# The up projection of a feed-forward part by Strassen's scheme, in quarters with the down projection

## The chip, the cores and the metric

The kernel runs on one core of a Trainium2 chip. The metric is the device time of one execution in microseconds. Engines are called TensorE (PE in the rows, PEld for its weight loads), VectorE (DVE), ScalarE (ACT), GpSimd (POOL) and SyncE (SP, which issues the loads and stores).

## What is computed

Two layers of an encoder trunk work on 512 tokens of 1024 features, all in float32. The change concerns the feed-forward part that ends each layer:

```python
D_MODEL, SEQ, DEPTH, D_FF = 1024, 512, 2, 4096
...
    for l in range(DEPTH):
        ...
        x = x + merged @ w_out[l]

        h = rms_norm(x, norm_ffn[l])
        x = x + jnp.square(jax.nn.relu(h @ w_ff1[l])) @ w_ff2[l]
```

`merged` is what three attention branches give, gated and summed; its product with `w_out` is the output projection that stands right before the feed-forward part.

## The kernel before

Activations lie feature-major: a tile has 128 features on the partitions and all 512 tokens in its columns, so x is 8 tiles. Every float32 product is made of three matmuls in the float32r type. Each operand is split into a rounded part `hi` and a remainder `lo`, and the three products hi·hi, hi·lo and lo·hi are added up in PSUM. `feature_tile` (line 324) issues these three matmuls for each of the k-tiles of one output tile; each matmul loads a 128x128 block of weights and moves 512 columns. The third of the three is the one that reads the weights' `lo`.

Weights come from one packed array through `Stream.take` (line 127). It loads 128x1024 numbers (eight 128x128 blocks) into a `raw` tile, makes `hi` by a ScalarE copy (line 140) and `lo` by a VectorE subtract (line 142). The tags `raw`, `whi` and `wlo` have three buffers each (pool `w`, line 185). The order of instructions on TensorE is that of the program; on the other engines a scheduler orders them by priority, and the instructions of `take` are moved ahead by 30 places (`high_priority`).

In `merge` (line 880) eight output tiles `ps_o` are computed, each is added to its tile of x, and `norm_part` (line 262) multiplies x by the gain, splits it into `xgh` and `xgl` and adds its square to `acc` on GpSimd. The factor of the norm depends on the token alone; it is worked out later (`norm_sums`, `norm_rows`) and lies in `rb`.

In `ffn` (line 919) two halves follow one another. In each, 16 up tiles are computed (8 k-tiles x 3 = 24 matmuls each). Each goes through relu, the factor `rb` and the square, and is split into `ah` and `al`. Then 8 down tiles take the 16 as their k-tiles (48 matmuls each) and are added to x. The first ups run interleaved, seven of eight steps each, while the last x tile is still being normalized. PSUM has 8 banks: 3 `mm`, 2 `s`, 2 `pt`, 1 `y`.

## Time and profile before

| | |
|---|---|
| median of 3 runs | 1858.28 us (1857.52 to 1861.04) |
| profiled execution, its own time | 1858.96 us |
| its span, first to last instruction | 1856.9 us |
| mean granted TensorE clock | 0.993 |
| TensorE busy | 1801.5 us in 8496 matmuls |
| VectorE, ScalarE, GpSimd busy | 1088.9, 784.5, 311.4 us |

The span is what the rows of the trace cover; the time of the execution is 2.1 us longer. A busy engine is one that has an instruction in it; on TensorE successive matmuls overlap, so that the distance between their starts, not their listed length, is what each adds.

### The profile page before, as it was taken

How to read it: one execution, taken by the hardware profiler on the slowest of the kernel's cores; microseconds unless marked ns; L12 is line 12 of the kernel's file. 1: busy time of each engine (PE TensorE's matmuls, PEld its weight loads, DVE VectorE, ACT ScalarE, POOL GpSimd, SP SyncE). 2: the span in 40 equal slices, each digit the busy share in tenths (PEclk: the TensorE clock that was granted, in tenths of full speed). 3: DMA queues.
4: the chain of work that ended last, by engine and by line, in shares of the span. 5: the costliest groups of instructions: out<-in, count | busy, mean ns of one | idle time of the engine just before them, and what ended most of it. 6: DMA issues, size and time to landing. Idle time of an engine off the chain costs nothing.

```text
span 1856.9 us, 23295 instructions
## 1 busy us (share of the span) xinstructions
PE 1801.5 (97%) x8496; PEld 1495.0 (81%) x8496; DVE 1088.9 (59%) x2223; ACT 784.5 (42%) x1369; POOL 311.4 (17%) x289
## 2 busy tenths in 40 slices
PE   8989989989999999999999899899899999999999
PEld 6778878877888888888887788788778888888887
DVE  7566468488865642454355654684888756334632
ACT  6565456446643221223245644564466433222221
POOL 1442222043101000000124312220431110000000
PEclk9999999999999999999999999999899999999999
DMA  5653365332252333333336533643322533333341
GB/s 180 154 147 105 101 163 138 100 113 69 80 193 80 106 99 98 96 100 110 119 113 158 132 96 109 169 116 110 103 84 80 178 95 97 102 91 102 92 119 62
DMA packets 78850, 211.46 MB, mean 114 GB/s; under 512 B 11392, under 2 KB 14464, under 8 KB 78736
## 3 DMA queue, kind: packets, MB, share of 16 engines
q1 hardware_dynamic: 78736, 209.97, 39.3%
q8 instruction: 67, 1.10, 0.2%
q14 instruction: 47, 0.39, 0.1%
HBM read 172.15 MB, written 12.62 MB: 100 GB/s over the span
## 4 chain that ended last, share of the span: by engine, by line
PE 79%; DVE 8%; ACT 4%; DMA 4%; issue 3%; POOL 2%; SPq 1%; DVEq 0%; ACTq 0%; POOLq 0%
PE ps L331 38%; PE ps_t L366 15%; PE ps_f L331 10%; PE ps_o L331 5%; PE ps_b L776 5%; PE ps_s L662 2%; PE ps_p L689 2%; PE ps_y L700 2%; DMA qq<-nat 2%; DVE pr L677 1%; POOL wlo L142 1%; DVE pr L670 1%; ACT whi L140 1%; DMA cb<-cum 1%; ACT pr L675 1%
## 5 line engine op out<-in xcount | busy, mean ns | idle before, releaser
L140 ACT ACTIVATE whi<-raw 128x1024 fp32r<-128x1024 f32 (+1 forms) x337 | 307.1, 919 | 764.8 <-issue 320.6
L142 DVE TENSOR_TENSOR wlo<-raw,whi 128x1024 fp32r<-128x1024 f32 (+2 forms) x237 | 287.6, 1213 | 232.2 <-ACT whi L140 227.8
L331 PE MATMUL ps<-xgh,whi 128*128 128x512 f32 x512 | 199.4, 389 | 0.0
L331 PE MATMUL ps<-xgh,wlo 128*128 128x512 f32 x512 | 199.2, 389 | 0.0
L331 PE MATMUL ps<-xgl,whi 128*128 128x512 f32 x512 | 199.2, 389 | 0.0
L331 PE MATMUL ps<-ah,whi 128*128 128x512 f32 x512 | 199.2, 389 | 0.0
L331 PE MATMUL ps<-al,whi 128*128 128x512 f32 x512 | 199.2, 389 | 0.0
L331 PE MATMUL ps<-ah,wlo 128*128 128x512 f32 x512 | 199.2, 389 | 0.0
L331 PE MATMUL ps_f<-xgh,whi 128*128 128x512 f32 x464 | 196.2, 423 | 0.0
L331 PE MATMUL ps_f<-xgh,wlo 128*128 128x512 f32 x464 | 182.5, 393 | 0.0
L331 PE MATMUL ps_f<-xgl,whi 128*128 128x512 f32 x464 | 182.5, 393 | 0.0
L142 POOL TENSOR_TENSOR wlo<-raw,whi 128x1024 fp32r<-128x1024 f32 x50 | 121.1, 2422 | 257.0 <-ACT whi L140 234.3
L366 PE MATMUL ps_t<-whi,xgh 128*128 128x512 f32 x384 | 151.2, 394 | 7.0 <-ACT whi L140 7.0
L366 PE MATMUL ps_t<-wlo,xgh 128*128 128x512 f32 x384 | 150.1, 391 | 0.0
L366 PE MATMUL ps_t<-whi,xgl 128*128 128x512 f32 x384 | 149.9, 390 | 0.0
L283 POOL TENSOR_TENSOR acc<-acc,t 128x512 f32<-128x512 f32 x24 | 41.6, 1732 | 518.9 <-ACT t L282 518.9
L331 PEld LDWEIGHTS ps<-ah,whi 128*128 128x128 f32 x512 | 96.1, 188 | 20.1
L331 PEld LDWEIGHTS ps<-xgl,whi 128*128 128x128 f32 x512 | 96.1, 188 | 19.9
L331 PEld LDWEIGHTS ps<-xgh,wlo 128*128 128x128 f32 x512 | 96.1, 188 | 19.9
L331 PEld LDWEIGHTS ps<-al,whi 128*128 128x128 f32 x512 | 96.1, 188 | 19.9
L331 PEld LDWEIGHTS ps<-xgh,whi 128*128 128x128 f32 x512 | 96.1, 188 | 19.9
L331 PEld LDWEIGHTS ps<-ah,wlo 128*128 128x128 f32 x512 | 96.1, 188 | 19.8
(194 smaller groups left out, 3387.0 us busy)
## 6 DMA issues: line engine op xcount, KB each, us to landing
raw<-w SPq DMA_DIRECT2D x277, 512.0 KB, 3.6
qq<-nat SPq DMA_DIRECT2D x64, 128.0 KB, 2.9
kk<-nat SPq DMA_DIRECT2D x64, 128.0 KB, 2.4
kl<-nat SPq DMA_DIRECT2D x64, 128.0 KB, 2.4
gd<-t SPq DMA_DIRECT2D x32, 256.0 KB, 2.2
cb<-cum SPq DMA_DIRECT2D x16, 256.0 KB, 4.0
cb<-gd SPq DMA_DIRECT2D x16, 256.0 KB, 2.7
g<-gd SPq DMA_DIRECT2D x16, 256.0 KB, 4.3
```

Of the source, the lines that this page charges most:

```text
L140: nc.scalar.activation(out=hi[:, c : c + v], in_=raw[:, c : c + v], func=AF.Copy)
L142: k.lo_engine.tensor_tensor(out=lo[:, c : c + w], in0=raw[:, c : c + w], in1=hi[:, c : c + w].bitcast(F32), op=ALU.subtract)
L283: (engine or nc.gpsimd).tensor_tensor(out=self.acc, in0=self.acc, in1=sq, op=ALU.add)
L331: nc.tensor.matmul(out=ps, lhsT=a[:, k], rhs=b[k], start=first and k == 0 and j == 0, stop=last and k == n - 1 and j == 2)
L366: nc.tensor.matmul(out=pss[t][:, 0:width], lhsT=a[k][:, t * P : t * P + P], rhs=b[:, i], start=c == 0 and i == 0 and j == 0, stop=last and ...
L662: nc.tensor.matmul(out=ps[:, 0:n], lhsT=a[:, i * P : (i + 1) * P], rhs=b[:, 0:n], start=j == 0, stop=j == len(terms) - 1)
L670: nc.vector.tensor_tensor_reduce(out=p, in0=ps[:, 0:n], in1=b, scale=1.0, scalar=-3e38 * sign, op0=ALU.add, op1=ALU.max if branch == 2 els ...
L675: nc.scalar.activation(out=p, in_=p, func=AF.Exp, bias=mn, scale=sign, accum_out=ls)
L677: nc.vector.tensor_scalar(out=p, in0=p, scalar1=li, scalar2=None, op0=ALU.mult)
L689: nc.tensor.transpose(ps[:, o + (i - kb) * P : o + (i - kb + 1) * P], pr[:, offs[i] + kb * P : offs[i] + (kb + 1) * P], self.ident)
L700: nc.tensor.matmul(out=yps[:, kb * P : T], lhsT=qkv[2][kb // 2][:, kb % 2, h, :], rhs=head[h][gi][x][:, o : o + T - kb * P], start=gi == 0 ...
L776: nc.tensor.matmul(out=pss[u], lhsT=chunk[a][:, u, k], rhs=y[b][k], start=k == 0 and j == 0, stop=k == 3 and j == 2)
```

## The change

The up projection is computed by Strassen's scheme in Winograd's form. The 1024 features are cut into two halves of 512, the 512 tokens into two halves of 256, and two up tiles (256 columns of `w_ff1`) form a pair, whose two column blocks are 128 wide. Each block product of 512 features x 128 columns x 256 tokens is 4 k-tiles x 3 = 12 matmuls of 256 columns. Seven such products replace the eight of a pair. Before them come sums of weight blocks (`take_pair`: four GpSimd subtracts and four splits, two of which go to tags `twh` and `twl` with two buffers) and sums of activation blocks (`norm_pair`, in place of `norm_part`; the output tiles are computed in the order 0, 4, 1, 5, ...). After them come the sums of products in `pair_sum`.

`ffn` runs in four quarters: four pairs (8 up tiles), then 8 downs over 8 k-tiles (24 matmuls each), each added to x. The factor of the norm is squared (`rb2`) and multiplied in after the downs. The weights of a pair are taken one pair ahead; those of the first pair of a later quarter are taken before the fifth down of the quarter ahead of it. The packing of `w_ff1` follows (`chunk_of`). Lines that are only "..." stand for parts left out.

```diff
+    def take_pair(self, pool, *key):
+        k, nc = self.k, self.k.nc
+        raw = [k.pw.tile([P, 1024], F32, tag="raw", name="raw") for _ in range(2)]
+        sums = [pool.tile([P, 1024], F32, tag="tw", name="tw", bufs=3) for _ in range(2)]
+        w = {}
+        def split(names, src, n, tags):
+            hi, lo = (p.tile([P, 1024], F32R, tag=t, name=t, **b) for p, t, b in tags)
+            nc.scalar.activation(out=hi[:, 0:n], in_=src[:, 0:n], func=AF.Copy)
+            nc.vector.tensor_tensor(out=lo[:, 0:n], in0=src[:, 0:n], in1=hi[:, 0:n].bitcast(F32), op=ALU.subtract)
+            for i, name in enumerate(names):
+                w[name] = tuple(x[:, 512 * i : 512 * i + 512].rearrange("p (k m) -> p k m", m=P) for x in (hi, lo))
+        with k.tc.high_priority(k.ahead):
+            for i in range(2):
+                nc.sync.dma_start(out=raw[i], in_=self.ap[self.layer, :, self.at + 1024 * i : self.at + 1024 * i + 1024])
+            b = [raw[i][:, 512 * j : 512 * j + 512] for i in range(2) for j in range(2)]
+            t = [sums[i][:, 512 * j : 512 * j + 512] for i in range(2) for j in range(2)]
+            sub = lambda out, x, y: nc.gpsimd.tensor_tensor(out=out, in0=x, in1=y, op=ALU.subtract)
+            plain = ((k.pw, "whi", {}), (k.pw, "wlo", {}))
+            summed = ((pool, "twh", dict(bufs=2)), (pool, "twl", dict(bufs=2)))
+            split(["b11"], raw[0], 512, plain)
+            split(["b21", "b22"], raw[1], 1024, plain)
+            sub(t[0], b[1], b[0])
+            sub(t[1], b[3], t[0])
+            split(["t1", "t2"], sums[0], 1024, summed)
+            sub(t[2], b[3], b[1])
+            sub(t[3], b[2], t[1])
+            split(["t3", "t4"], sums[1], 1024, summed)
+        self.at += 2048
+        self.keys.append((2048, key))
         return w
...
-        return dict(s=self.pS, y=self.py, mm=self.mm)[tag].tile([P, T], F32, tag=tag, name=name)
+        return dict(s=self.pS, y=self.py, mm=self.mm, pt=self.pt)[tag].tile([P, T], F32, tag=tag, name=name)
...
+    def norm_pair(self, l, vcol, pool, kt, x):
+        nc = self.nc
+        h2 = T // 2
+        a, b = slice(0, h2), slice(h2, T)
+        g = self.gain(l, vcol + kt)
+        if kt < 4:
+            self.half = self.half if kt else {}
+            t = self.half[kt] = self.tmp()
+            nc.scalar.activation(out=t, in_=x, func=AF.Copy, scale=g)
+            return
+        t = self.half.pop(kt - 4)
+        q = pool.tile([P, 3, h2], F32, tag="sq", name="sq", bufs=1)
+        sub = lambda out, u, v: nc.vector.tensor_tensor(out=out, in0=u, in1=v, op=ALU.subtract)
+        h = self.px.tile([P, T], F32R, tag="xgh", name="xgh")
+        lo = self.px.tile([P, T], F32R, tag="xgl", name="xgl")
+        nc.scalar.activation(out=h, in_=x, func=AF.Copy, scale=g)
+        sub(q[:, 1], t[:, a], t[:, b])
+        nc.vector.scalar_tensor_tensor(out=t[:, b], in0=x[:, b], scalar=g, in1=t[:, b], op0=ALU.mult, op1=ALU.add)
+        sub(q[:, 0], t[:, b], t[:, a])
+        nc.vector.scalar_tensor_tensor(out=q[:, 2], in0=x[:, a], scalar=g, in1=q[:, 0], op0=ALU.mult, op1=ALU.subtract)
+        nc.vector.scalar_tensor_tensor(out=lo, in0=x, scalar=g, in1=h.bitcast(F32), op0=ALU.mult, op1=ALU.subtract)
+        f = {"a12": [y[:, a] for y in (h, lo)], "a22": [y[:, b] for y in (h, lo)]}
+        h = self.px.tile([P, T], F32R, tag="xgh", name="xgh")
+        lo = self.px.tile([P, T], F32R, tag="xgl", name="xgl")
+        nc.scalar.activation(out=h, in_=t, func=AF.Copy)
+        sub(lo, t, h.bitcast(F32))
+        f |= {"a11": [y[:, a] for y in (h, lo)], "s1": [y[:, b] for y in (h, lo)]}
+        h = pool.tile([P, 3, h2], F32R, tag="sh", name="sh", bufs=4)
+        lo = pool.tile([P, 3, h2], F32R, tag="sl", name="sl", bufs=4)
+        nc.scalar.activation(out=h, in_=q, func=AF.Copy)
+        sub(lo, q, h.bitcast(F32))
+        for i in range(3):
+            f[f"s{2 + i}"] = [y[:, i] for y in (h, lo)]
+        self.xf.append(f)
...
-    def norm_rows(self):
-        nc = self.nc
-        ps = self.pt.tile([P, T], F32, tag="pt", name="ps_r")
+    def norm_rows(self, tag=None):
+        nc = self.nc
+        ps = self.bank(tag, "ps_r") if tag else self.pt.tile([P, T], F32, tag="pt", name="ps_r")
...
-    def merge(self, l, y, x):
+    def merge(self, l, y, x, pool):
...
-                self.norm_part(l, V_FFN, m, x[m])
-
-            outs = [out(m) for m in range(KT)]
+                self.norm_pair(l, V_FFN, pool, m, x[m])
+                self.norm_square(m, x[m])
+            self.xf = []
+            outs = [out(m) for m in (0, 4, 1, 5, 2, 6, 3, 7)]
...
+    PRODUCTS = (
+        ("b11", "a11", 0, 0),
+        ("b21", "a12", 1, 0),
+        ("t2", "s2", 1, 1),
+        ("t3", "s3", 2, 0),
+        ("t1", "s1", 2, 1),
+        ("t4", "a22", 3, 0),
+        ("b22", "s4", 3, 1),
+    )
+    def pair_products(self, w, tags, order):
+        nc = self.nc
+        h2 = T // 2
+        ps = [None] * 4
+        for i in order:
+            stationary, moving, bank, half = self.PRODUCTS[i]
+            if ps[bank] is None:
+                ps[bank] = self.bank(tags[bank], f"ps_w{bank}")
+            out = ps[bank][:, half * h2 : half * h2 + h2]
+            hi, lo = w[stationary]
+            n = len(self.xf)
+            for k, f in enumerate(self.xf):
+                xh, xl = f[moving]
+                for j, (a, b) in enumerate(((hi, xh), (hi, xl), (lo, xh))):
+                    nc.tensor.matmul(out=out, lhsT=a[:, k], rhs=b, start=k == 0 and j == 0, stop=k == n - 1 and j == 2)
+            yield
+        self.ps = ps
+    def pair_sum(self, ps, z):
+        nc = self.nc
+        h2 = T // 2
+        add = lambda out, x, y: nc.vector.tensor_tensor(out=out, in0=x, in1=y, op=ALU.add)
+        two = lambda x: x.rearrange("p (u t) -> p u t", u=2)
+        p1 = self.tmp()[:, 0:h2]
+        nc.scalar.activation(out=p1, in_=ps[0][:, 0:h2], func=AF.Copy)
+        add(z[:, 0:5:4], two(ps[1]), p1.unsqueeze(1).to_broadcast([P, 2, h2]))
+        add(z[:, 5:7], two(ps[2]), z[:, 4].unsqueeze(1).to_broadcast([P, 2, h2]))
+        add(z[:, 3], ps[2][:, h2:T], z[:, 5])
+        add(z[:, 1:3], two(ps[3]), z[:, 5:7])
+        return z[:, 0:4].rearrange("p (u v) t -> p u (v t)", u=2)
     def ffn(self, l, x):
         nc = self.nc
         with ExitStack() as ctx:
-            pa = self.pool(ctx, "act", 16)
-            xg = self.nx
-
-            def up(f, out):
-                hi, lo = self.streams[l].take(1024, "f1", f)
-                ps = self.bank("s" if f == 3 else "mm", "ps_1")
-                yield from self.feature_tile(ps, [c.rearrange("p (k m) -> p k m", m=P) for c in (hi, lo)], *xg)
+            pa = self.pool(ctx, "act", 4)
+            pf = self.pool(ctx, "ffn", 1)
+            take = lambda j: self.streams[l].take_pair(pf, "f1", j)
+            def up(j, w, a):
+                order = (0, 1, 5, 3, 4, 2, 6) if j == 0 else range(7)
+                yield from self.pair_products(w, (("y", "mm", "mm", "mm"), ("s", "s", "pt", "pt"))[j % 2], order)
+                c = self.pair_sum(self.ps, pf.tile([P, 7, T // 2], F32, tag="z", name="z"))
+                nc.scalar.activation(out=c, in_=c, func=AF.Relu)
+                nc.scalar.activation(out=c, in_=c, func=AF.Square)
+                h, lo = pa.tile([P, 2, T], F32R, tag="ah", name="ah"), pa.tile([P, 2, T], F32R, tag="al", name="al")
+                nc.scalar.activation(out=h, in_=c, func=AF.Copy)
+                nc.vector.tensor_tensor(out=lo, in0=c, in1=h.bitcast(F32), op=ALU.subtract)
+                for u in range(2):
+                    a[0].append(h[:, u])
+                    a[1].append(lo[:, u])
+            def down(q, m, a):
+                ps = self.mm.tile([P, T], F32, tag="mm", name="ps_2")
+                w = self.streams[l].take(1024, "f2", 8 * q, m)
+                yield from self.feature_tile(ps, [c.rearrange("p (k m) -> p k m", m=P) for c in w], *a)
                 t = self.tmp()
-                nc.vector.scalar_tensor_tensor(out=t, in0=ps, scalar=0.0, in1=self.rb, op0=ALU.max, op1=ALU.mult)
-                h = pa.tile([P, T], F32R, tag="ah", name="ah")
-                lo = pa.tile([P, T], F32R, tag="al", name="al")
-                nc.scalar.activation(out=h, in_=t, func=AF.Square)
-                nc.vector.tensor_tensor(out=t, in0=t, in1=t, op=ALU.mult)
-                nc.vector.tensor_tensor(out=lo, in0=t, in1=h.bitcast(F32), op=ALU.subtract)
-                out[0].append(h)
-                out[1].append(lo)
-
-            for half in range(2):
+                nc.vector.tensor_tensor(out=t, in0=ps, in1=rb2, op=ALU.mult)
+                nc.vector.tensor_tensor(out=x[m], in0=x[m], in1=t, op=ALU.add)
+                if q == 3:
+                    if l + 1 < DEPTH:
+                        nc.sync.dma_start(out=self.xd[:, m], in_=x[m])
+                        self.norm_part(l + 1, V_MIX, m, x[m])
+                    else:
+                        nc.sync.dma_start(out=self.a["out"][:, m], in_=x[m])
+            w = take(0)
+            for q in range(4):
                 a = ([], [])
-                ups = [up(16 * half + f, a) for f in range(16)]
-                if half == 0:
-                    for u in ups[0:2]:
-                        for _ in range(7):
-                            next(u)
-                    self.norm_sums()
-                    next(ups[0])
-                    next(ups[1])
-                    for _ in range(7):
-                        next(ups[2])
-                    self.norm_rows()
-                    next(ups[2])
-                    for _ in range(7):
-                        next(ups[3])
-                for u in ups:
-                    run_all(u)
-                if half == 1 and l + 1 < DEPTH:
+                for j in range(4 * q, 4 * q + 4):
+                    ahead = take(j + 1) if j % 4 < 3 else None
+                    run_all(up(j, w, a))
+                    w = ahead
+                    if j == 0:
+                        self.norm_sums()
+                    if j == 1:
+                        self.norm_rows("mm")
+                        rb2 = pf.tile([P, T], F32, name="rb2")
+                        nc.vector.tensor_tensor(out=rb2, in0=self.rb, in1=self.rb, op=ALU.mult)
+                if q == 3 and l + 1 < DEPTH:
                     self.norm_begin()
-                for m in range(KT):
-                    ps = self.mm.tile([P, T], F32, tag="mm", name="ps_2")
-                    for c in range(2):
-                        hi, lo = self.streams[l].take(1024, "f2", 16 * half + 8 * c, m)
-                        run_all(self.feature_tile(ps, [w.rearrange("p (k m) -> p k m", m=P) for w in (hi, lo)], a[0][8 * c : 8 * c + 8], a[1][8 * c : 8 * c + 8], first=c == 0, last=c == 1))
-                    nc.vector.tensor_tensor(out=x[m], in0=x[m], in1=ps, op=ALU.add)
-                    if half == 1:
-                        if l + 1 < DEPTH:
-                            nc.sync.dma_start(out=self.xd[:, m], in_=x[m])
-                            self.norm_part(l + 1, V_MIX, m, x[m])
-                        else:
-                            nc.sync.dma_start(out=self.a["out"][:, m], in_=x[m])
+                downs = [down(q, m, a) for m in range(KT)]
+                for d in downs[0:2]:
+                    for _ in range(6):
+                        next(d)
+                for i, d in enumerate(downs):
+                    if i == 4 and q < 3:
+                        w = take(4 * q + 4)
+                    run_all(d)
...
-                self.merge(l, y, x)
+                ps = self.pool(xctx, "sums", 1, side="right")
+                self.merge(l, y, x, ps)
...
-        c = pk(i["w_ff1"][l][:, key[1] * P : (key[1] + 1) * P])
+        w = i["w_ff1"][l][:, 2 * key[1] * P : (2 * key[1] + 2) * P]
+        c = np.stack([pk(w[512 * r : 512 * r + 512, P * u : P * u + P]) for r in range(2) for u in range(2)], axis=1)
```

## Rows read from the trace of the kernel before

**Rows 1.** The page: engines' busy time, chain that ended last, weight loads.

```profile
PE 1801.5 (97%) x8496; PEld 1495.0 (81%) x8496; DVE 1088.9 (59%) x2223; ACT 784.5 (42%) x1369; POOL 311.4 (17%) x289
...
PE 79%; DVE 8%; ACT 4%; DMA 4%; issue 3%; POOL 2%; SPq 1%; DVEq 0%; ACTq 0%; POOLq 0%
...
raw<-w SPq DMA_DIRECT2D x277, 512.0 KB, 3.6
```

**Rows 2.** Windows of layer 0: first half's downs, second half's ups.

```profile
core 0: us, PE busy (x) PEld busy (x) DVE busy (x) ACT busy (x) POOL busy (x), PEclk, DMA share, GB/s
...
667.40:754.40 87.00, 87.00 (x385) 72.08 (x384) 26.39 (x26) 17.52 (x18) 0.00 (x0) 1.00 0.32 97
754.40:841.40 87.00, 87.00 (x385) 72.07 (x384) 50.09 (x62) 24.76 (x31) 0.00 (x0) 1.00 0.32 97
```

**Rows 3.** Groups of instructions, second half's ups; the first line names columns.

```profile
line engine op names shapes xcount | busy us, mean ns | idle before us <-releasers
...
L142 DVE TENSOR_TENSOR wlo<-raw,whi 128x1024 fp32r<-128x1024 f32 x16 | 19.6, 1225 | 3.5 <-ACT whi L140 3.5
L140 ACT ACTIVATE whi<-raw 128x1024 fp32r<-128x1024 f32 x16 | 17.0, 1062 | 62.8 <-issue 54.1 <-PE ps L331 8.8
L935 DVE TENSOR_TENSOR al<-t,ah 128x512 fp32r<-128x512 f32 x15 | 10.4, 693 | 0.5
```

**Rows 4.** Timeline of TensorE, narrow matmuls: start us, length us, what ran.

```profile
304.22 0.28 PE L662 MATMUL ps_s<-kk,qq 128*128 128x256 f32 x1
304.33 0.28 PE L662 MATMUL ps_s<-kl,qq 128*128 128x256 f32 x1
304.45 0.40 PE L331 MATMUL ps_f<-xgh,whi 128*128 128x512 f32 x1
...
307.47 0.22 PE L662 MATMUL ps_s<-kk,qq 128*128 128x128 f32 x1
307.53 0.27 PE L662 MATMUL ps_s<-kl,qq 128*128 128x128 f32 x1
307.63 0.45 PE L700 MATMUL ps_y<-ptl,v 128*128 128x384 f32 x2
...
1426.54 0.52 PE L662 MATMUL ps_s<-st 96*128 96x256 f32 x3
1426.89 0.40 PE L700 MATMUL ps_y<-pth,v 128*128 128x512 f32 x1
```

**Rows 5.** Timeline at the end of the last down of a half.

```profile
754.40 1.06 ACT L140 ACTIVATE whi<-raw 128x1024 fp32r<-128x1024 f32 x1 [4.38 <-PE ps L331]
754.42 0.39 PE L331 MATMUL ps<-xgh,whi 128*128 128x512 f32 x1
...
754.62 0.69 DVE L964 TENSOR_TENSOR x<-x,ps 128x512 f32<-128x512 f32 x1 [3.35 <-PE ps L331]
...
754.88 0.39 PE L331 MATMUL ps<-xgh,wlo 128*128 128x512 f32 x1
...
755.49 1.23 DVE L142 TENSOR_TENSOR wlo<-raw,whi 128x1024 fp32r<-128x1024 f32 x1 [0.18 <-ACT whi L140]
```

**Rows 6.** Timeline at the end of the output projection.

```profile
578.80 0.39 PE L331 MATMUL ps<-xgh,whi 128*128 128x512 f32 x1
...
579.00 0.69 DVE L908 TENSOR_TENSOR x<-x,ps_o 128x512 f32<-128x512 f32 x1 [2.63 <-PE ps_o L331]
...
579.79 0.71 ACT L271 ACTIVATE xgh<-x,vec 128x512 fp32r<-128x512 f32 x1
```

**Rows 7.** Timeline of VectorE and GpSimd in the output projection.

```profile
548.16 0.75 DVE L272 SCALAR_TENSOR_TENSOR xgl<-x,vec,xgh 128x512 fp32r<-128x512 f32 x1
...
549.96 1.78 DVE L272 SCALAR_TENSOR_TENSOR xgl<-x,vec,xgh 128x512 fp32r<-128x512 f32 x1
...
549.86 1.33 POOL L283 TENSOR_TENSOR acc<-acc,t 128x512 f32<-128x512 f32 x1 [63.19 <-ACT t L282]
```

**Rows 8.** Groups of GpSimd instructions; columns as in rows 3.

```profile
L283 POOL TENSOR_TENSOR acc<-acc,t 128x512 f32<-128x512 f32 x24 | 41.6, 1732 | 518.9 <-ACT t L282 518.9
```

More of the change, by code (lines that the diff above doesn't have):

```diff
@@ L125, in take_stacked @@
         return w
+    def take_pair(self, pool, *key):
[27 more added lines that the diff above has]
+        self.keys.append((2048, key))
+        return w
     def take(self, n, *key, pieces=1):
```

## The prediction

> **What bounds the kernel now.** I read the page's totals and chain first, then the feed-forward stage in windows, then single instructions. TensorE is busy for 97% of the span and the chain that ended last is mostly its own [rows 1]. Inside the feed-forward part it never stops: a half of 16 up tiles or of 8 down tiles takes 87.0 us at full granted clock (1.00, the 2.4 GHz level) with 384 matmuls in it, while VectorE is busy 50 us beside the ups and 26 beside the downs, and ScalarE 25 and 18 [rows 2]. 87.0 / 384 = 0.2267 us from one 512-column matmul to the next; the listed length of a matmul (0.39) is no price, since matmuls overlap. So a matmul removed gives 0.227 us back, and a new operation elsewhere costs only where TensorE must wait for it. What it may have to wait for is weights: each 128x1024 weight tile needs a ScalarE copy (1.06) and a VectorE subtract (1.225) before use [rows 3]. The tiles live in three buffers (pool `w`, line 185), and that shows: ScalarE starts the next split only when TensorE has left a tile, after 4.38 us of idling [rows 5]. That split is for two tiles later, so TensorE feels nothing.
>
> **The up products.** The downs keep their 1536 matmuls, in other groups. Removed: 64 column tiles x 24 = 1536 matmuls of 512 columns, 1536 x 0.2267 = 348.2 us. Added: 32 pairs x 7 products x 12 = 2688 matmuls of 256 columns, each with its own weight load. The trace has 256-column ones: two in a row take 0.23 us (304.22 to 304.45, the second 0.12), three in a row 0.35 (1426.54 to 1426.89), so 0.115 to 0.120 each [rows 4]. I take 0.118: 317.2 us, a gain of **31.0**; the ends 0.115 and 0.120 give 39.1 and 25.6. The 128-column ones warn: the second takes 0.10, not 0.06 [rows 4]; a matmul doesn't go faster than its weights come, at about 0.10. 256 columns lie just above.
>
> The Trainium skill (TensorE: Matmul & The Clock Gate, Back-to-back issue gap) puts the gap at N/2.4 + 2.5 ns, which as an estimate makes 109 ns of 256 columns and 216 of 512, so 331.3 us before, 293.5 after and a gain of 37.8 in place of 31.0. The trace has 227 for 512, so I stay with the rows.
>
> **The seams between quarters.** `take(4q+4)` now stands before the fifth of the eight downs (`i == 4`), for q = 0, 1, 2. Its two plain tiles (b11; b21 with b22) come out of the same three `whi`/`wlo` buffers as the downs' weights, and are held until the next up runs, after the last down. One buffer is left. The fifth down gets its buffer beside them; the sixth, seventh and eighth can be split only when the one before has left the buffer: three handovers per seam, 3 x 3 seams x 2 layers = 18. The price of one can be read at a tile's end [rows 5]: TensorE starts the following tile at 754.42, ScalarE's split for the freed buffer starts 754.40, VectorE evacuates 754.62 to 755.31 and subtracts 755.49 to 756.72. Today this serves a later tile; in a handover the very next tile waits for it. Its third matmul is the first that reads wlo, due at 754.88; it would start at about 756.8, **1.9 us late**. The downs also get a second evacuation op (`x += t`, 0.69 as for any 128x512 [rows 3]); in front of the subtract it makes 2.45. Behind the waiting subtract stands only that evacuation. I take 2.2: 18 x 2.2 = **39.6 us** (34.2 to 44.1). If the fifth down also comes behind the pair's tiles there are four per seam, 24 x 2.2 = 52.8, at most 58.8.
>
> **Into the feed-forward part.** Before, the first two ups ran seven of eight steps each while the last x tile was normalized. Now every product needs all four k-tiles, and the fourth exists only after the last output tile. By today's times [rows 6]: TensorE is through at 578.80, x is added 579.00 to 579.69, and xgh takes 0.71 from 579.79. On VectorE follow three 256-column ops (0.35 to 0.45 each, half of 0.69 and a little), a split of 0.75 [rows 7] and the a11 split of 0.69: 582.3. TensorE has work for 10 matmuls, to 579.98. So 2.4 us of standing still, 3.0 if the next pair's b11 subtract (0.69) comes in between: 2 x 3.0 = **6.0** (3 to 8).
>
> **VectorE and GpSimd.** A pair now takes 84 x 0.118 = 9.9 us. In it VectorE has 0.69 + 3 x 1.225 weight subtracts, 1.225 for `lo` of the result and four additions out of PSUM (3 x 0.69 + 0.4), 8.1 us; ScalarE about 6.5 (3.5 weight copies and 3 passes over z, at 1.06 per 1024, less for the small ones); GpSimd four subtracts. GpSimd takes 1.33 for 128x512 [rows 7], 1.73 on average [rows 8]. Alone all fit. But a VectorE op that began 0.1 us after a GpSimd one took 1.78 instead of 0.75 and ended 0.55 after it [rows 7]: it stood still meanwhile. Subtracts with both inputs in SBUF are 5.6 us of VectorE's 8.1, and 5.6 + 4 x 1.33 = 10.9 exceeds 9.9. A quarter softens it: only three pairs' weights are made during its four ups (39.6 us). VectorE: 3 x 4.37 weights + 4 x 2.5 additions + 4 x 1.225 results + 2 x 1.225 for the first downs = 30.5; 12 GpSimd ops, if VectorE stands through two thirds of each, 10.6 more: 41.1, 1.5 over. Half gives 38.5, no loss; all of each 46.5, 6.9 over. Times 8 quarters: 0, 12 or 55; two buffers of sums made ahead take some off, and I take **9**.
>
> The Trainium skill (SBUF — State Buffer, Who interferes with whom) says that a VectorE instruction with two SBUF inputs and a GpSimd instruction that reads SBUF exclude each other, whichever began first blocking the other for its whole length. The trace agrees with its 1.78.
>
> **The end.** The last down has two VectorE ops instead of one before its store: **0.7**, once; after layer 0 the next mixer's first tiles cover it (else 1.4).
>
> **At nothing:** the weight bytes and their loads (a load lands in 3.6 us [rows 1], less than a down tile, and is issued tiles ahead; the pair's two stand before the fifth down's on SP's queue, which has nothing else to issue there); rb2 and the row matmuls, first needed after four pairs, 40 us (uncovered 2 us); the second evacuation elsewhere (VectorE is idle 3.35 us before each one [rows 5]); the last pair's chain of additions, relu, square, copy and subtract, about 0.7 + 3.2 + 1.2 = 5 us, covered by the first downs' 36 matmuls on older results, 8.2 us (uncovered 5 x 8 = 40).
>
> **Sum.** -31.0 + 39.6 + 6.0 + 9 + 0.7 = +24.3 on the profiled execution's 1858.96 (span 1856.9, 2.1 around it; 0.7 above the median): **1883**.
>
> **Rivals.** *No handovers, faster:* the last downs' weights are ready in time. For: every split now starts two tiles early [rows 5]. Against: three buffers, two of them held. Then -31 + 6 + 0.7 + 0 to 9: 1835 to 1844, say 1839. It decides when a handover costs under (31 - 6 - 0.7 - 9) / 18 = 0.85 us, or when fewer than 7 of 18 occur. 0.20. *Four handovers:* 13.2 more, 1896; the order on one buffer decides. 0.18. *The shared port binds the ups:* 55 for 9, 1929; for it speaks 10.9 over 9.9, against it the work done ahead. 0.10. *The seven products are no cheaper than eight:* at 348.2 / 2688 = 0.1295 us a matmul nothing is gained: 31 more, 1914. For: 0.10 at 128 columns; against: three in a row at 0.117 [rows 4]. 0.05. *Everything at its cheap end:* -39.1 + 34.2 + 3 + 0 + 0.7 = -1, 1858. 0.05. My forecast has 0.42, with a range of its own from 1868 to 1900.
>
> **Chances and range.** What a measurement can't tell from no change is 0.2%, 3.7 us. Faster: 0.20 and part of the cheap case, 0.22; same 0.04; slower 0.74. From 1838 to 1925 is left out half of the case without handovers (0.10), half of the bound port and a little above (0.08).
>
> **What would show it.** Right: products spaced 0.118 without gaps; about 18 stops of 2 us in the down stages of the first three quarters, TensorE waiting for `wlo` at the start of the last downs, ScalarE's `whi` there waiting for TensorE; a stop of 2 to 3 us before each feed-forward part; VectorE subtracts stretched beyond 1.225 in the ups. Wrong: downs at 5.44 us throughout (then it is faster), or products above 0.13, or stops inside the ups on `twl` of some us per pair.

## The result, and the profile after

The changed kernel takes 1980.26 us (median of 4 runs, 1973.39 to 1985.66) against 1857.90 for the kernel before on the same chip: a ratio of 1.0653, 95% interval [1.0614, 1.0693]. It is slower, as forecast, but far above the 1883 us and above the range's upper end of 1925. The profiled execution took 1976.95 us, its span 1975.2: 118.3 more than before. The page of the changed kernel, against [rows 1]:

```profile
PE 1826.6 (92%) x9648; PEld 1547.5 (78%) x9648; DVE 1280.9 (65%) x2393; ACT 919.9 (47%) x1513; POOL 503.1 (25%) x417
```

And the groups of down matmuls, with columns as in [rows 3]:

```profile
L404 PE MATMUL ps<-ah,wlo 128*128 128x512 f32 x512 | 212.9, 416 | 31.1 <-DVE wlo L178 31.1
L404 PE MATMUL ps<-ah,whi 128*128 128x512 f32 x512 | 212.8, 416 | 29.5 <-ACT whi L176 22.1 <-ACT ah L1053 7.4
```

TensorE's share fell from 97% to 92%, and the down matmuls (line 404 now) have idle time in front of them whose releasers are mostly the splits of weights (the 7.4 on `ah` are late results, below). The feed-forward part of layer 0, cut at its quarters (ups, then downs, four times; columns as in [rows 2]):

```profile
580.50:637.40 56.90, 44.43 (x347) 43.56 (x346) 47.30 (x60) 27.25 (x33) 26.38 (x17) 0.88 0.30 87
637.40:700.70 63.30, 50.28 (x195) 37.78 (x194) 26.54 (x30) 14.93 (x15) 13.34 (x9) 0.92 0.24 73
700.70:741.90 41.20, 40.64 (x338) 40.40 (x337) 31.37 (x32) 23.29 (x27) 11.81 (x7) 1.00 0.33 97
741.90:799.40 57.50, 49.34 (x194) 37.66 (x194) 24.50 (x29) 13.12 (x13) 11.62 (x9) 0.94 0.26 78
799.40:841.35 41.95, 40.90 (x338) 40.45 (x337) 32.14 (x32) 23.29 (x27) 12.17 (x8) 1.00 0.32 96
841.35:903.90 62.55, 51.84 (x194) 39.31 (x193) 26.60 (x29) 13.13 (x13) 12.83 (x9) 0.89 0.24 71
903.90:945.85 41.95, 40.87 (x338) 40.42 (x337) 32.10 (x32) 23.28 (x27) 11.36 (x7) 1.00 0.32 94
945.85:989.50 43.65, 43.65 (x196) 36.14 (x195) 26.76 (x34) 20.28 (x25) 9.23 (x6) 1.00 0.45 138
sum 409.00, PE 361.95 PEld 315.73 DVE 247.31 ACT 158.57 POOL 108.75; mean PE 45.24 PEld 39.47 DVE 30.91 ACT 19.82 POOL 13.59
```

Before, a quarter's ups or downs would be 43.5 us (half of 87.0, [rows 2]). (Lengths of stages in the text below are taken from the first to the last start of a matmul, 0.1 to 0.2 us less than in the windows.) Three kinds of row stand out. The last quarter's downs, which have no quarter behind them, take 43.65: they are undisturbed. The other downs take 57.5 to 63.3 and the first ups 56.9, and these are the rows with a granted clock under 1. The remaining ups take 41.2 to 41.95, less than 43.5, which is the gain that the scheme has to offer. A handover, in which one down tile passes its weight buffer to the very next one, in the middle of the first seam; TensorE, its weight loads, ScalarE and VectorE:

```profile
667.25 0.39 PE L404 MATMUL ps<-ah,wlo 128*128 128x512 f32 x1
667.45 1.06 ACT L176 ACTIVATE whi<-raw 128x1024 fp32r<-128x1024 f32 x1 [4.38 <-PE ps L404]
667.67 0.69 DVE L1064 TENSOR_TENSOR t<-ps,rb 128x512 f32<-128x512 f32 x1 [2.89 <-PE ps L404]
668.40 0.69 DVE L1065 TENSOR_TENSOR x<-x,t 128x512 f32<-128x512 f32 x1
...
668.55 0.19 PEld L404 LDWEIGHTS ps<-ah,whi 128*128 128x128 f32 x1 [1.34 <-ACT whi L176]
668.55 0.50 PE L404 MATMUL ps<-ah,whi 128*128 128x512 f32 x1 [0.92 <-ACT whi L176]
...
668.89 0.40 PE L404 MATMUL ps<-al,whi 128*128 128x512 f32 x1
669.01 1.22 DVE L178 TENSOR_TENSOR wlo<-raw,whi 128x1024 fp32r<-128x1024 f32 x1
...
670.28 0.50 PE L404 MATMUL ps<-ah,wlo 128*128 128x512 f32 x1 [0.99 <-DVE wlo L178]
```

ScalarE's 4.38 us of idling before the split are those of [rows 5], only that the very next tile needs the result now. From 667.25 to 668.55 TensorE waits for `whi` (1.30 from start to start), and from 668.89 to 670.28 for `wlo` (1.39), because two evacuation ops stand in front of the subtract. Less the two normal distances of 0.227 that is 2.24 us. This happens at the fifth, sixth, seventh and eighth down of each seam: four times, 24 in all. The entry into the feed-forward part, VectorE, GpSimd and the two stops of TensorE:

```profile
579.84 4.19 POOL L148 TENSOR_TENSOR tw<-raw 128x512 f32<-128x512 f32 x3
...
581.49 0.28 PE L1021 MATMUL ps_w<-xgh,wlo 128*128 128x256 f32 x1
...
582.84 1.48 DVE L331 SCALAR_TENSOR_TENSOR t<-x,vec,t 128x256 f32<-128x256 f32 x1
...
584.24 1.75 DVE L334 SCALAR_TENSOR_TENSOR xgl<-x,vec,xgh 128x512 fp32r<-128x512 f32 x1
...
588.73 3.42 DVE L139 TENSOR_TENSOR twl<-tw,twh 128x1024 fp32r<-128x1024 f32 x2
...
588.77 0.58 PE L1021 MATMUL ps_w<-xgh,whi 128*128 128x256 f32 x1 [7.00 <-ACT xgh L338]
...
592.07 1.74 DVE L326 TENSOR_TENSOR xgl<-t,xgh 128x512 fp32r<-128x512 f32 x1
...
593.87 0.58 PE L1021 MATMUL ps_w<-xgl,whi 128*128 128x256 f32 x1 [4.52 <-DVE xgl L326]
...
594.25 0.42 PE L1021 MATMUL ps_w<-xgh,wlo 128*128 128x256 f32 x1
```

TensorE stands 7.28 and then 5.10 us from start to start, 12.1 more than normal. The ops of the last x tile are stretched while GpSimd makes sums (1.48 for a 128x256 op, 1.75 for an `xgl` that took 0.75 alone, [rows 7]), and two splits of weight sums (3.42) stand in front of the last `xgl`. After the stop the products follow at 0.21 us (19 in 4.00 us in the second window below), not 0.12. The granted clock goes with it, in windows after this stop:

```profile
588.70:594.00 5.30, 0.71 (x2) 0.42 (x2) 5.30 (x5) 0.86 (x2) 4.07 (x3) 0.50 0.22 83
594.00:598.00 4.00, 4.00 (x19) 4.00 (x20) 3.98 (x2) 1.44 (x2) 3.92 (x3) 0.51 0.46 135
598.00:602.00 4.00, 4.00 (x36) 4.00 (x35) 0.45 (x1) 1.06 (x1) 1.14 (x1) 1.00 0.45 131
```

0.50 is the 1.2 GHz level: in 594 to 598 TensorE never idles and still does 19 matmuls where the next 4 us hold 36. In the third seam (841.35 to 903.90), where no late result adds to the handovers, the granted clock is 0.89 on average.

**The ledger.** The two feed-forward parts take 409.0 and 411.6 us. Before, each took 349.7, 699.4 in all, so they are 121.2 longer. That is more than eight times 87.0, since the first ups of a layer held the norm's row matmuls already, as this row of the kernel before shows (columns as in [rows 2]):

```profile
578.70:667.40 88.70, 88.70 (x397) 73.36 (x396) 53.47 (x85) 26.53 (x34) 1.79 (x1) 1.00 0.32 95
```

The rest of the span is 2.9 shorter: 1.7 longer ahead of layer 0's feed-forward part, 5.4 shorter between the layers, 0.8 longer at the end. I summed the distances between successive starts of TensorE against 0.120 (products) and 0.2267 (downs):

| part | us |
|---|---|
| products at 0.120 instead of ups at 0.2267 | -25.6 |
| 24 handovers x 2.24 | +53.8 |
| handovers longer than that, and other short waits in the seams | +8.0 |
| results of the last pair late, first seam of each layer (6.1 + 6.2) | +12.3 |
| 115 down matmuls at the lower clock (0.43 us apart) | +24.0 |
| the one matmul after each stop (0.34 instead of 0.227) | +8.2 |
| entry, xgh and xgl (2 x 12.1) | +24.3 |
| waits for twl and the like inside the ups | +11.3 |
| 57 products at the lower clock (0.21 us apart) | +5.4 |
| row matmuls of the norm among the first ups (2.6 instead of 2.8) | -0.2 |
| sum | +121.5 |

### The profile page after: what moved, and what is told of

It reads as the page before. It is cut to its first block, busy times and chain, and to the rows that moved or that the text cites. A ratio compares the mean times of both kernels' runs of the same rounds, so it can differ in the third digit from the quotient of the medians.

```text
span 1975.2 us, 26259 instructions
## 1 busy us (share of the span) xinstructions
PE 1826.6 (92%) x9648; PEld 1547.5 (78%) x9648; DVE 1280.9 (65%) x2393; ACT 919.9 (47%) x1513; POOL 503.1 (25%) x417
## 5 line engine op out<-in xcount | busy, mean ns | idle before, releaser
L176 ACT ACTIVATE whi<-raw 128x1024 fp32r<-128x1024 f32 (+3 forms) x273 | 238.1, 884 | 456.7 <-PE ps L404 195.6
L178 DVE TENSOR_TENSOR wlo<-raw,whi 128x1024 fp32r<-128x1024 f32 (+3 forms) x173 | 215.2, 1247 | 89.8 <-ACT whi L176 80.9
L404 PE MATMUL ps<-ah,wlo 128*128 128x512 f32 x512 | 212.9, 416 | 31.1 <-DVE wlo L178 31.1
L148 POOL TENSOR_TENSOR tw<-raw 128x512 f32<-128x512 f32 x64 | 91.8, 1436 | 365.8 <-DMA raw<-w 284.4
L1064 DVE TENSOR_TENSOR t<-ps,rb 128x512 f32<-128x512 f32 x64 | 44.1, 690 | 205.4 <-PE ps L404 205.4
L404 PEld LDWEIGHTS ps<-ah,wlo 128*128 128x128 f32 x512 | 102.0, 199 | 64.6 <-DVE wlo L178 43.3
L148 POOL TENSOR_TENSOR tw<-raw,tw 128x512 f32<-128x512 f32 x64 | 108.1, 1689 | 137.2 <-DMA raw<-w 137.0
L139 DVE TENSOR_TENSOR twl<-tw,twh 128x1024 fp32r<-128x1024 f32 x64 | 94.8, 1486 | 41.5 <-ACT twh L138 41.4
L748 ACT ACTIVATE pr<-pr,mn 128x512 f32<-128x512 f32 (+3 forms) x128 | 71.5, 559 | 80.9 <-DVE mn L743 75.8
L138 ACT ACTIVATE whi<-raw 128x512 fp32r<-128x512 f32 x64 | 54.1, 845 | 110.6 <-PE ps L404 67.7
L138 ACT ACTIVATE twh<-tw 128x1024 fp32r<-128x1024 f32 x64 | 66.7, 1055 | 80.0 <-PE ps_w L1021 42.9
```

The lines of the kernel that those rows point to most:

```text
L138: nc.scalar.activation(out=hi[:, 0:n], in_=src[:, 0:n], func=AF.Copy)
L139: nc.vector.tensor_tensor(out=lo[:, 0:n], in0=src[:, 0:n], in1=hi[:, 0:n].bitcast(F32), op=ALU.subtract)
L148: sub = lambda out, x, y: nc.gpsimd.tensor_tensor(out=out, in0=x, in1=y, op=ALU.subtract)
L176: nc.scalar.activation(out=hi[:, c : c + v], in_=raw[:, c : c + v], func=AF.Copy)
L178: k.lo_engine.tensor_tensor(out=lo[:, c : c + w], in0=raw[:, c : c + w], in1=hi[:, c : c + w].bitcast(F32), op=ALU.subtract)
L404: nc.tensor.matmul(out=ps, lhsT=a[:, k], rhs=b[k], start=first and k == 0 and j == 0, stop=last and k == n - 1 and j == 2)
```

## The experiments

Each stands against the kernel before on its own chip, where that had a median of 1854.3 to 1859.8 us; so between chips the ratios are to be compared. The first four start from the changed kernel.

**The pair's weights after the downs' (`e1_order`).** The next quarter's first pair is taken when the eighth down has got its weights.

```diff
-                    if i == 4 and q < 3:
+                    if i == 7 and q < 3:
+                        next(d)
                         w = take(4 * q + 4)
```

> The next quarter's first pair is taken after the eighth down has taken its weights, in place of before the fifth. Theory A (buffers): the four handovers per seam come from the pair's two plain tiles holding two of the three weight buffers. Then the 24 handovers of 2.24 us (53.8 us) go, and with them most of the half clock that follows the stops (20 to 25 us more): 1890 to 1910, downs of quarters 1 and 2 at 5.44 us each. Rival B (shared port): the weights of the last downs are late because VectorE and GpSimd exclude each other; then the sums only move and the time stays within 10 us of 1980. Rival C: the pair now comes too late, and what the downs win is lost at the start of the next quarter's first up: about 1950 to 1980.

Measured: 1879.51 us (1879.18 to 1882.88), ratio 1.0120 [1.0105, 1.0135]. The downs of layer 0's first two quarters:

```profile
639.05:687.10 48.05, 45.88 (x194) 36.98 (x194) 26.24 (x30) 14.91 (x15) 9.23 (x7) 0.96 0.30 90
...
728.35:771.85 43.50, 43.50 (x194) 36.03 (x194) 24.66 (x29) 13.26 (x13) 9.50 (x7) 1.00 0.31 96
```

All handovers are gone, and the later seams run at 43.5 with a clock of 1.00. The place of the take alone cost 101 us of the 122, 11 more than was expected at most. In the sums of distances, stops in the downs go from 74.1 to 5.2 us, matmuls at the lower clock from 24.0 to 3.0, and those behind a stop from 8.2 to 1.2. The late results are in the first of these: they fall from 12.3 to 5.2, so about 7 of the 101 are theirs. The low clock went with the stops, though nothing else was done about it.

**b11 in tiles of its own (`e2_b11`).** The order stays, but the pair's smaller plain tile leaves the three buffers.

```diff
-            hi, lo = (p.tile([P, 1024], F32R, tag=t, name=t, **b) for p, t, b in tags)
+            hi, lo = (p.tile([P, 512 if t[0] == "b" else 1024], F32R, tag=t, name=t, **b) for p, t, b in tags)
...
-            split(["b11"], raw[0], 512, plain)
+            split(["b11"], raw[0], 512, ((pool, "bwh", {}), (pool, "bwl", {})))
```

> Nothing moves in the order; only b11 gets two buffers of its own (half size, one each), so that a pair holds one of the three weight buffers and the downs keep two. Theory A (buffers): two are enough, since a split takes 2.3 us of a down's 5.44; the handovers go as in the other experiment, 1890 to 1910. Rival B (shared port) or a rival in which the early place of the pair's instructions delays the downs' splits: no change beyond 10 us.

Measured: 1884.51 us (1882.95 to 1886.05), ratio 1.0143 [1.0128, 1.0158].

```profile
641.15:690.60 49.45, 46.90 (x194) 37.99 (x193) 30.13 (x31) 14.90 (x15) 13.95 (x9) 0.93 0.30 87
...
731.65:775.70 44.05, 43.81 (x194) 35.93 (x194) 27.15 (x30) 13.58 (x13) 13.22 (x9) 1.00 0.34 98
```

One buffer more for the downs is enough, with the take and all its instructions where they were. Four of the six seams keep one wait for `wlo` of 0.6 to 1.3 us from start to start, and the first ups of a layer get longer (59.0 and 59.1 us instead of 56.8 and 57.7), which the gain in the seams hides. So it is the buffers, not the pair's loads or VectorE's load at the seam, that made the handovers.

**The first pair by k-tiles (`e3_entry`).** Three products run over the first three k-tiles before any needs the fourth.

```diff
-                order = (0, 1, 5, 3, 4, 2, 6) if j == 0 else range(7)
+                order = range(7)
+                cuts = [(i, (0, 3)) for i in (0, 1, 6)] + [(i, (3, 4)) for i in (1, 0, 6)] + [(i, (0, 4)) for i in (2, 4, 3, 5)]
...
```

> In the first pair of each layer three products run over their first three k-tiles before any of them needs the fourth: 27 matmuls, 3.2 us of work in place of 1.1, and the products that need weight sums come last. If the stop there is TensorE waiting for the fourth x tile alone, it shrinks by 2.1 us and by part of the half clock behind it, twice: 1972 to 1977. If VectorE as a whole is behind there (theory B), the later products wait instead, and the time stays within 3 us of 1980.

Measured: 1969.14 us (1964.84 to 1976.50), ratio 1.0603 [1.0574, 1.0631]. The first ups go from 56.8 and 57.7 us to 55.5 and 55.3. That is 3.8 us of the 11 between the medians; the late results shrink too, from 12.3 us to 7.7, and the executions of either kernel differ by about 12 us among themselves. The time is below both of the expected ranges, so only the rows decide. More covered work at the start buys little: the stops come back later (2.3, 2.5 and 5.1 us on `xgl`, `xgh`, `xgl`). What is late is the production of the last activations, not the order in which they are used.

**GpSimd without its sums (`e4_memset`).** The four subtracts become fills, so the weight sums are left out of the computation; the splits of the filled tiles stay.

```diff
-            sub = lambda out, x, y: nc.gpsimd.tensor_tensor(out=out, in0=x, in1=y, op=ALU.subtract)
+            sub = lambda out, x, y: nc.gpsimd.memset(out, 0.5)
```

> GpSimd's four subtracts per pair are replaced by memsets of the sums' tiles (the sums are left out; GpSimd reads nothing there and doesn't wait for the loads). Theory B (shared port): VectorE's two-input ops go back from 1.5 to 0.69 and from 1.5 to 1.225 us, the stop before the first pair shrinks from 12.4 us to about 5, the stops on the weight sums inside the ups (about 1.1 to 2 us per quarter) go, and the late results at the first seam of each layer (6 us) shrink: 1925 to 1950. Theory A (buffers): the 24 handovers stay at 2.24 us each. If the port costs nothing: within 5 us of 1980.

Measured: 1928.46 us (1926.21 to 1931.45), ratio 1.0385 [1.0368, 1.0402]. Windows of layer 0 as above, then VectorE at the entry:

```profile
581.50:630.55 49.05, 44.46 (x347) 43.97 (x346) 35.17 (x61) 29.44 (x35) 13.43 (x23) 0.93 0.30 91
630.55:691.30 60.75, 51.16 (x194) 38.69 (x193) 23.95 (x29) 12.32 (x13) 1.67 (x4) 0.92 0.23 70
691.30:731.65 40.35, 40.35 (x338) 40.31 (x337) 29.34 (x35) 25.67 (x29) 6.08 (x13) 1.00 0.35 105
```

```profile
580.77 2.85 POOL L148 MEMSET tw<- 128x512 f32 x6
...
582.89 0.48 DVE L331 SCALAR_TENSOR_TENSOR t<-x,vec,t 128x256 f32<-128x256 f32 x1
583.29 0.74 DVE L334 SCALAR_TENSOR_TENSOR xgl<-x,vec,xgh 128x512 fp32r<-128x512 f32 x1
```

Beside fills VectorE's ops have their undisturbed lengths (0.48 instead of 1.48, 0.74 instead of 1.75). The later ups have no stop at all (40.35), and the first ups lose 7.8 and 9.6 us. The 24 handovers stand as before (1.31 and 1.39 each): GpSimd has no part in them, only in stretching some. The late results at the first seams shrink from 6.1 and 6.2 us to 2.4 each. The fills also don't wait for the weights' loads, which this experiment doesn't keep apart.

**Priority for the last x tile (`e5_prio`)**, on top of the new order (`e1_order`):

```diff
-                self.norm_pair(l, V_FFN, pool, m, x[m])
+                with self.tc.high_priority(400 if m == 7 else 1):
+                    self.norm_pair(l, V_FFN, pool, m, x[m])
```

> On top of taking the next pair after the last down's weights (1879.5 us): the ops that normalize the last x tile go ahead of weight splits in the queues. Theory A (order of VectorE's queue): of the 12.4 us stop before the first pair about 5 us are weight subtracts that stand in VectorE's queue ahead of the last tile's ops (one of b11, 1.6 us, two of the sums, 3.4 us). Then the stop shrinks by 4 to 5 us per layer, with part of the half clock behind it: 1866 to 1871. Theory B (the work itself, stretched by the shared port): the weights' splits are needed as soon as the tile, and TensorE waits for them instead: over 1876.

Measured: 1867.33 us (1866.34 to 1868.38), ratio 1.0060 [1.0046, 1.0074].

```profile
584.25 0.58 PE L1022 MATMUL ps_w<-xgh,whi 128*128 128x256 f32 x1 [3.33 <-ACT xgh L338]
588.28 0.58 PE L1022 MATMUL ps_w<-xgl,whi 128*128 128x256 f32 x1 [3.46 <-DVE xgl L326]
```

The stops shrink from 7.28 and 5.10 to 3.60 and 4.04: the weight splits ahead in VectorE's queue were a part of the entry. The stretched ops stay (1.48, 1.75, 1.48, 1.75 in a row).

**Quarters alone (`e6_quarters`).** The kernel before with four quarters of its ordinary products instead of two halves.

```diff
-            for half in range(2):
+            for half in range(4):
...
-                ups = [up(16 * half + f, a) for f in range(16)]
+                ups = [up(8 * half + f, a) for f in range(8)]
```

> The kernel before with four quarters in place of two halves, and nothing else: the ordinary eight block products, no sums. If the quarters by themselves cost nothing (TensorE has the same matmuls, the downs' evacuations are hidden in 5.44 us each): 1856 to 1861. If the shorter groups make TensorE wait at each change from ups to downs: 1 to 2 us at 8 changes, 1866 to 1874.

Measured: 1854.37 us (11 runs, 1848.21 to 1857.85), ratio 0.9993 [0.9981, 1.0005]. Quarters by themselves cost nothing that can be measured: each feed-forward part takes 349.7 us, as with halves.

**All repairs together (`e7_combo`)**: new order, priority, the first pair by k-tiles, and three downs instead of two begun on older results in the first quarter.

```diff
-                for d in downs[0:2]:
+                for d in downs[0 : 2 if q else 3]:
```

> The changed kernel with the next pair taken after the last down's weights, the last x tile's ops first in the queues, the first pair of a layer working on three k-tiles of three products before any fourth one, and three downs (not two) begun before the last pair's results in the first quarter. Theory A: 1879.5 less 10 to 14 at the layer's entry and less 9 at the first seams: 1855 to 1861, about as before. Theory B (the sums' work on VectorE and GpSimd is the limit, and a stop that is closed opens at the next product): over 1868.

Measured: 1861.54 us (1860.05 to 1864.17), ratio 1.0033 [1.0020, 1.0047]. The downs of the first seam fall from the 47.9 us of `e1_order` to 43.6, so the late results are covered by 18 matmuls more. The first ups stay at 55.0 and 54.5: with the priority in place, the order by k-tiles adds next to nothing.

**New order and no sums (`e8_clean`)**: `e1_order` with the fills of `e4_memset`; the sums are left out again.

> The next pair is taken after the last down's weights, and GpSimd's four subtracts per pair are memsets (the sums are left out). Theory A plus B: no handovers, no stretched VectorE ops: 1879.5 less 17 at the entries (8.5 per layer, as the memsets gave) and less 9 on the weight sums in the ups: 1849 to 1855. If the two effects overlap: over 1860. What is left below 1858 is what seven products could win with the sums for nothing but their splits.

Measured: 1845.47 us (1843.91 to 1847.86), ratio 0.9943 [0.9930, 0.9957]. Every stage except the first ups (48.3, 48.7) and first downs (45.8, 45.9) of a layer runs at 40.2 or 43.3 without a stop.

**The sums on VectorE (`e9_first`, `e10_vector`)**, on top of `e7_combo`: those of the first two pairs of a layer, or all of them.

```diff
-            sub = lambda out, x, y: nc.gpsimd.tensor_tensor(out=out, in0=x, in1=y, op=ALU.subtract)
+            sub = lambda out, x, y: (nc.vector if key[1] < 2 else nc.gpsimd).tensor_tensor(out=out, in0=x, in1=y, op=ALU.subtract)
```

> On top of the combined kernel (1861.5 us): the weight sums of the first two pairs of each layer are made on VectorE in place of GpSimd. Theory B (shared port): a sum costs VectorE 0.69 us of its own, but a GpSimd subtract beside it holds it for 1.3 to 2; near the entry eight sums change places, so VectorE wins about 5 us there per layer, and the first ups shrink from 55 to about 50 us: 1851 to 1855. If the amount of VectorE's work is the limit and not the exclusion: 1861 or more.

> All sums on VectorE, GpSimd makes none. Theory B (shared port): VectorE's work per quarter's ups is 30.5 + 12 x 0.69 = 38.8 us of TensorE's 40.3, so it just fits; nothing is stretched, the stops on the weight sums (1 to 2 us per quarter) go: 1843 to 1850. If VectorE becomes the limit: stops of 2 to 4 us in every quarter, 1865 to 1885.

Measured: first two pairs 1857.52 us (12 runs, 1853.47 to 1861.24), ratio 1.0014 [1.0003, 1.0025]; all 1858.02 (12 runs, 1853.60 to 1862.41), ratio 1.0019 [1.0007, 1.0031]. With the first two pairs' sums there, the first ups fall from 55.0 and 54.5 us to 51.8 and 52.0, while the other ups keep their waits. With all sums on VectorE the first ups fall to 49.4 and 50.5 us and the other ups to 40.2, without a stop. It gives this back in the six later down stages, 45.1 instead of 43.3, by stops of 0.9 on `ah` and 1.3 on `al`: with more work in VectorE's queue the last pair's results come late there too, as the next experiment tests. Both times lie between the two outcomes that had been expected.

**Three downs begun in every quarter (`e11_three`)**, on top of all sums on VectorE:

```diff
-                for d in downs[0 : 2 if q else 3]:
+                for d in downs[0:3]:
```

> The kernel with all sums on VectorE (e10_vector), and three downs begun before the last pair's results are needed in every quarter, not in the first alone. In e10_vector six down stages took 45.1 us instead of 43.3, by stops of 0.85 on ah and 1.26 on al at their start. Theory: those stops are lateness of the last pair's results, and 18 more matmuls (4.1 us) on older results cover them: the six stages come to 43.3 to 43.6, about 10 us less in all, 1846 to 1850, a ratio of 0.995 to 0.998. Rival: the third down's weights need a buffer that the last pair still holds, and the stops only move to its start: stages at 45 or above, 1856 or more, a ratio of 1.000 to 1.005.

Measured: 1851.16 us (6 runs, 1846.36 to 1852.17), ratio 0.9949 [0.9933, 0.9965]. Layer 0's first two quarters:

```profile
582.40:633.65 51.25, 45.96 (x347) 44.75 (x346) 43.76 (x75) 26.64 (x33) 1.44 (x1) 0.90 0.34 103
633.65:678.20 44.55, 43.83 (x195) 35.99 (x194) 29.62 (x38) 14.64 (x15) 0.00 (x0) 1.00 0.31 94
678.20:718.55 40.35, 40.35 (x338) 40.31 (x337) 30.06 (x38) 22.57 (x27) 0.00 (x0) 1.00 0.36 106
718.55:762.05 43.50, 43.50 (x194) 36.04 (x194) 29.56 (x38) 13.92 (x14) 0.00 (x0) 1.00 0.32 97
```

The stops were lateness of the results, and 4.1 us of older work cover it in the six later down stages, which come to 43.3; the third down's weights are in time. This version leaves nothing out and is faster than both kernels, by 0.5% than the one before. The later stages have no stop left. VectorE's busy time in a quarter's ups is 30.1 us in 38 instructions, less than the 31 to 32 of the changed kernel in 32, though it makes the sums as well: GpSimd is idle there and nothing stretches it. What remains is the entry, 51.2 and 50.6 us in place of some 41, and a stop of about 1 us on `al` in the first downs of a layer.

## Why the prediction was right or wrong

**Where the difference lies.** The forecast was 24.3 us on the span and 118.3 came. By the ledger, 54.4 of the 94.0 between them lie in the seams, 18.3 in the entry and 5.4 in the products at the lower clock, 12.3 in the late results, 5.4 in the price of a product, 2.3 in the waits inside the ups; the rest of the span gave some 4 back.

**What bounds it, and the direction: right.** TensorE's stream sets the time, and the losses were waits of TensorE in it, the lower clock behind them and the dearer products. Slower was the larger chance and came.

**The up products: right, at the dear end.** Successive products start 0.120 us apart (median of 2658 pairs), so the gain is 25.6, the lower end given, not 31.0:

```profile
704.89 0.28 PE L1021 MATMUL ps_w<-sl,twh 128*128 128x256 f32 x1
705.01 0.28 PE L1021 MATMUL ps_w<-sh,twl 128*128 128x256 f32 x1
```

The Trainium skill's formula (TensorE: Matmul & The Clock Gate, Back-to-back issue gap), which is stated there for an isolated matmul, made 109 ns as an estimate; the trace disagrees by 11 ns, as it did at 512 columns.

**The seams: mechanism and price right, the count one short, and its consequences not priced.** The handover was read from [rows 5] at 2.2 us and took 2.24. There were four per seam, not three: the pair's splits went in front of the fifth down's, which the rival of four handovers had. `e1_order` and `e2_b11` show the cause, buffers that the pair holds, from two sides. The step that failed is "18 x 2.2": it had a handover too few in each seam, and it charged each stop only for its own length. Behind a stop the first matmul took 0.34, and among the repeated stops the granted clock fell to its 1.2 GHz level for stretches, in which the down matmuls came 0.43 apart. With the stretched ones among them the handovers cost 94 us by the ledger (53.8 + 8.0 + 24.0 + 8.2; the late results' own share of the low clock is in it), where 39.6 was put down, and taking them away gave 101, some 7 of it from the late results. [rows 2] show a clock of 1.00 for stages in which TensorE never stood; [rows 4] to [rows 6] hold no row of a matmul after a stop.

**The entry: mechanism right, size wrong.** 3.0 us per layer was put down and 12.1 came. The step that failed is the chain of VectorE ops costed at undisturbed lengths. The prediction used the exclusion of [rows 7] for the ups but not here, where GpSimd makes the first pairs' sums at the same moment: `e4_memset` brings the two stops to 2.21 and 3.04, about 5.0 net. The queue was the other part: the splits of weight sums in front of the last `xgl` (`e5_prio`: 7.28 + 5.10 to 3.60 + 4.04). The parts overlap, and each experiment removes some of the other's. 57 products ran at the lower clock as well, 5.4 us for which the prediction had no term.

**VectorE and GpSimd: about right.** 9 was taken for stops inside the ups; 11.3 came, most of it as waits of 0.5 to 1.2 us for `twl`, one or two in each quarter's ups. They vanish without GpSimd's reads (`e4_memset`) and when VectorE makes the sums (`e10_vector`). The busy time shows it as well: `twl` took 1.49 us on average instead of 1.225. The rule of the Trainium skill that was weighed there (SBUF — State Buffer, Who interferes with whom) names only a GpSimd instruction that reads SBUF, not one that merely writes; the trace agrees, since beside fills VectorE's ops kept 0.48 and 0.74.

**At nothing: one item was wrong.** The last pair's results were to be covered by the first downs' 36 matmuls. At the first seam of each layer they came 6.1 and 6.2 us late:

```profile
647.67 1.06 ACT L138 ACTIVATE twh<-tw 128x1024 fp32r<-128x1024 f32 x1 [1.03 <-POOL tw L148]
648.64 1.04 ACT L1053 ACTIVATE ah<-z 128x1024 fp32r<-128x1024 f32 x1
...
649.90 2.29 DVE L1054 TENSOR_TENSOR al<-z,ah 128x1024 fp32r<-128x1024 f32 x1
```

ScalarE waits for GpSimd's sum of the next pair with the finished `z` queued behind it, and the subtract of `al` is then stretched to 2.29. The chain had been added up by lengths, without what stands in front of it in the queues. `e1_order`, which takes the next pair later, brings the 6.1 and 6.2 to 2.6 each. Of the uncovered price of 40 us given for all eight quarters, 12.3 came.

**The end** (0.7 put down): the evacuation is two ops of 0.69, and the time behind the last matmul grew by 0.8.

**The rivals.** Without handovers the time was to be 1839; `e1_order` has none and takes 1879.51, because entry, late results and the ups' waits cost more than put down there. It is neared only where the sums are out as well (`e8_clean`, 1845.47) or on VectorE with their seams covered (`e11_three`, 1851.16). Four handovers was right about the count, with 1896 too low by the clock and the entry. The bound port and the products at no gain did not come.

**Left open.** What shortens the stretch between the layers by 5.4 us: `e6_quarters`, with ordinary products, has it too (570.4 us against 574.8 before, one trace each), so the new products need not be the cause. And which part of `e4_memset`'s gain at the entry is the loads' and which the exclusion's: in `e9_first` VectorE still waits for the loads and does more work, and the first ups fall by 3.2 and 2.5 us, so the exclusion has a part, whose size at the entry stays open.

## What to carry to other kernels

Before a prefetch is moved ahead of running work, count the buffers that it holds until its use: here two of three were gone, and one extra buffer or a later place was worth 96 to 101 us, four times what the arithmetic saved. A stop on the engine that sets the time costs more than its length when the engine comes back at a lower clock, as it did here, so price a chain of short stops with the matmuls behind them. Cost a latency chain with what stands ahead of it in each queue and with the neighbour that shares its port at that moment, not from undisturbed lengths.

## What the runs showed of the hardware

The granted clock fell among stops of 1.3 and 1.4 us, two in each handover of some 8 us, though not behind every one of them: in the second seam of layer 0 the windows of the four handovers have 1.00, 0.82, 0.82 and 1.00. Without the stops (`e1_order`) the same stage has 1.00 throughout.

```profile
765.60:773.50 7.90, 6.01 (x24) 4.35 (x24) 2.49 (x4) 1.03 (x2) 0.00 (x0) 1.00 0.35 117
773.50:783.10 9.60, 7.60 (x25) 5.53 (x25) 2.61 (x4) 1.09 (x2) 1.29 (x1) 0.82 0.19 55
783.10:792.60 9.50, 7.63 (x24) 5.49 (x24) 2.47 (x4) 1.06 (x1) 3.78 (x3) 0.82 0.18 55
792.60:799.40 6.80, 5.77 (x24) 4.48 (x25) 1.71 (x2) 0.00 (x0) 0.47 (x1) 1.00 0.27 80
```

The first matmul after a stop took 0.34 us to the next one instead of 0.227 even where the granted clock stayed at 1.00, as in the first of these windows. In the handover shown above the weight load and the matmul that follow a stop are listed from the same instant (668.55), whereas a load otherwise starts some 0.2 us ahead of its matmul (668.66 for that of 668.89). So the load that can't run ahead would account for the 0.11 us more; no run separates this.
